# Laying the far group's stationary blocks out side by side before a value projection

## The chip, the cores and the metric

The kernel runs on one core of one Trainium2 chip. The metric is device microseconds of one execution, the median of three runs. The program is about 17,000 instructions on five engines: TensorE (PE in the profile, with its weight loads as PEld), VectorE (DVE), the activation engine (ACT), GpSimd (POOL) and SyncE (SP), which only issues transfers.

## The reference, cut to what matters

One layer of an encoder block: a half-step SwiGLU feed-forward, a token mixing of two attention branches, and a second half-step feed-forward. The change sits in the mixing, in the values of the dilated attention branch:

```python
proj = h @ w_in[l]
qa, ka, va, qb, kb, vb, gate_a, gate_b = jnp.split(proj, splits, axis=-1)
...
def to_res(a):     # group g has dilation 1, 4 or 16
    return a.reshape(B, L, dilation, H, Dh).transpose(0, 2, 3, 1, 4).reshape(B * dilation, H, L, Dh)
o, lse = _banded_attention(to_res(q), to_res(k), to_res(v), half, dilation, slopes)
```

There are 512 tokens, 1024 channels, and three dilated groups of four heads of width 64. The kernel treats the groups with dilation 4 and 16 alike: tokens are sorted by their number modulo 4, four blocks of 128 tokens. These two are the far group.

## The kernel before, in words

Every product is made in three passes. A float32 operand is split into a high part (rounded to the fast matmul type) and a low part (the rest), and `mm3` (lines 203 to 206) issues high x high, high x low and low x high into one PSUM bank.

The normalised activations `hn` lie in SBUF with channels on the partitions, as eight chunks k = 0 to 7 of 128 channels by 512 tokens, one set of high parts (`hn_hi`) and one of low parts (`hn_lo`).

The mixing (lines 1255 to 1534) runs in this order on PE:

- the neighbourhood branch's query and key products, its value projection, its scores and its weighted sums;
- six dilated pairs (lines 1379 and 1380): pair j multiplies the activations with a query piece and a key piece, 24 matmuls each, into one bank each. `qk_parts` (line 974) then reads both banks on ACT and DVE and writes split copies. For pairs 2 to 5 it works through the 128 partitions in two halves, one for each of two heads: for each half ACT writes a scaled query (line 993), DVE its rest (line 994), and twice ACT a high part and DVE a low part of the key (lines 113 and 114, called by `split`), and two copies across (lines 999 and 1000). The query bank is free after the second half's line 994, and the key bank after the second half's last line 114;
- the far value projection `v_far` (line 1042), here called the far stage: 8 chunks k, 4 token blocks n, 3 passes, so 96 matmuls of 512 columns into four banks. The stationary operand is `seen(1, ...)` (line 935), a view of 128 tokens that stand four apart in memory. Two chunks share a weight piece (`take()`);
- the near value projection `v_near` (line 1016), then 16 gate projections with the remaining attention work beside them, and the output products.

In and around the far stage PE also runs the far groups' scores, `scores_narrow` (line 1098): each of eight heads uses two banks in turn, each filled by two matmuls (line 1106) and read by DVE (line 1110, then line 1114 twice).

All PSUM accumulators come from one pool of eight banks (line 56). While the far stage runs, four are its accumulators. Two others hold the products of pair 5 until `qk_parts` has read them, and two are left. A score that needs a third bank must take one from pair 5.

SBUF tiles of 128x512 float32 come from a pool of 38 units (line 53); a new tile waits until the last reader of the unit's former tile has run. The weight pieces arrive as `raw` tiles by SP and are split by ACT (line 113, 128x1024) and DVE (line 114, 128x1024) a few pieces ahead of their use.

In this part of the mixing the order of instructions on each engine is not written out by hand. A scheduler places them when the program is built, by program order, priorities and its own estimate of when operands are there. Each engine then runs its list in that order: an instruction that waits holds all behind it. Elsewhere (the feed-forwards, the start, the end) the order is pinned.

Of the kernel before, what the change touches and what calls it, by code (L numbers as in the profile page):

```python
# [12 lines left out]
F32 = mybir.dt.float32  # L13
F32R = mybir.dt.float32r
# [6 lines left out]
P = 128  # L21
T = 512
D = 1024
NK = D // P
# [9 lines left out]
URGENT = 400  # L34
# [12 lines left out]
def block_kernel(ctx, tc, x, gains, weights, rpb_near, rpb_all, alibi0, alibi12, out):  # L47
    nc = tc.nc
# [12 lines left out]
    def unit(dt=F32, name="u"):  # L61
        return up.tile([P, 512], dt, tag="u", name=name)
# [9 lines left out]
    def bank(name="ps"):  # L72
        return pp.tile([P, 512], F32, tag="ps", name=name)
# [15 lines left out]
    hn_hi, hn_lo = Rows(0), Rows(1)  # L89
# [30 lines left out]
    state = {"used": False, "next": 0, "take": 0, "stop": EARLY + 2 * STD, "ahead": lambda: None}  # L120
# [56 lines left out]
    def cut(w, c, n):  # L177

        return [a[c // 512][:, c % 512:c % 512 + n] for a in w]

    def take(ahead=True):
        w = pieces.pop(state["take"])
        state["take"] += 1
        if ahead:
            fill(NPIECE - 1)
        return w
# [11 lines left out]
    def step(n=1):  # L198
        for _ in range(n):
            if pend:  # L200
                pend.popleft()()

    def mm3(o, sh, sl, mh, ml, start, stop, **kw):
        nc.tensor.matmul(o, sh, mh, start=start, stop=False, **kw)  # L204
        nc.tensor.matmul(o, sh, ml, start=False, stop=False, **kw)  # L205
        nc.tensor.matmul(o, sl, mh, start=False, stop=stop, **kw)  # L206

    def proj_into(o, w, lo=0, hi=T):
        for k in range(NK):
            mm3(o[:, lo:hi], *cut(w, k * P, P),  # L210
                hn_hi[:, k, lo:hi], hn_lo[:, k, lo:hi], k == 0, k == NK - 1)
# [10 lines left out]
    def pair(use, j, n=2):  # L222
        a = bank()
        proj_into(a, take())
        step(n)
        b = bank()
        proj_into(b, take())
        step(n)
        use(j, a, b)
# [705 lines left out]
    def seen(kind, ap):  # L935

        if kind == "na":
            return ap.rearrange("p (r c) -> p c r", r=8)
        if kind == 0:
            return ap  # L940
        return ap.rearrange("p (i c) -> p c i", c=4)
# [18 lines left out]
    def parts_for(paired):  # L960
        if paired:
            t = twin("pair")
            return [t[:, cs] for cs in halves]
        return unit(F32R, "a"), unit(F32R, "a")

    def shaped(dst, view):
        sh = view.shape
        if len(sh) == 2:
            return dst
        if len(sh) == 3:  # L970
            return dst.rearrange("p (a b) -> p a b", a=sh[1])
        return dst.rearrange("p (a b c) -> p a b c", a=sh[1], b=sh[2])
# [31 lines left out]
    def v_parts(ps, v=None):  # L1004
        v = unit(F32R) if v is None else v
        v4 = v.rearrange("p (h s d) -> p h s d", h=4, s=2)
        split(v4[:, :, 0, :], v4[:, :, 1, :], ps.rearrange("p (h d) -> p h d", h=4))
        return v4
# [7 lines left out]
    def v_near():  # L1016
# [22 lines left out]
            step()  # L1039
        return [vv[3]] + vv[:3]  # L1040

    def v_far():

        acc = [bank() for _ in range(4)]
        for k in range(NK):
            if k % 2 == 0:
                w = take()
            parts = [seen(1, a[:, k, :]) for a in (hn_hi, hn_lo)]
            for n in range(4):
                mm3(acc[n], parts[0][:, n], parts[1][:, n], *cut(w, (k % 2) * 512, 512), k == 0, k == NK - 1)  # L1050
            if k % 2:
                step(2 if k == 5 else 1)
        vv = [[], []]
        for n in range(4):
            both = parts_for(True)
            for i in range(2):
                vv[i].append(v_parts(acc[n][:, i * 256:(i + 1) * 256], both[i]))
        return vv
# [196 lines left out]
    def mixing(g):  # L1255
# [9 lines left out]
        def load_tables(us, n, src):  # L1265
            def one(i):
                u = unit(name="table")
                nc.sync.dma_start(u, src[:, i * 512:(i + 1) * 512])
                us.append(u)
            for i in range(n):  # L1270
                loads.append(lambda i=i: one(i))
# [52 lines left out]
        def joint(g):  # L1324
            u = unit(name="joint")
            j = u[:, 0:96].rearrange("p (t g h c) -> p t g h c", t=4, g=3, h=4)
            nc.scalar.dma_start(u[:, 0:96].rearrange("p (t e) -> p t e", t=4), st_views[g])
            nm, rc, s = [u[:, 96 + 16 * i:112 + 16 * i].rearrange("p (t h) -> p t h", t=4) for i in range(3)]
            e, ws = [u[:, 144 + 48 * i:192 + 48 * i].rearrange("p (g t h) -> p g t h", g=3, t=4) for i in range(2)]
            nc.vector.tensor_tensor(nm, j[:, :, 0, :, 0], j[:, :, 1, :, 0], op=ALU.min)  # L1330
            nc.vector.tensor_tensor(nm, nm, j[:, :, 2, :, 0], op=ALU.min)
            for i in range(3):
                nc.vector.tensor_tensor(e[:, i], nm, j[:, :, i, :, 0], op=ALU.subtract)
            nc.scalar.activation(e, e, AF.Exp)
            nc.vector.tensor_tensor(ws, e, j[:, :, :, :, 1].rearrange("p t g h -> p g t h"), op=ALU.mult)
            nc.vector.tensor_tensor(ws[:, 0], ws[:, 0], ws[:, 1], op=ALU.add)
            nc.vector.tensor_tensor(ws[:, 0], ws[:, 0], ws[:, 2], op=ALU.add)
            nc.vector.reciprocal(rc, ws[:, 0])
            nc.vector.tensor_tensor(s, rc, e[:, g], op=ALU.mult)
            scl[g] = s  # L1340
# [36 lines left out]
        load_tables(g_tab[2], 1, alibi12[:, :512])  # L1377
        load_tables(g_tab[3], 1, alibi12[:, 512:])
        for j in range(6):
            pair(g_use, j, 1)  # L1380
        pend.append(lambda: joint(1))
        vvb[1], vvb[2] = v_far()
        vvb[0] = v_near()
        step(len(pend))
# [26 lines left out]
        parts = {}  # L1411
# [111 lines left out]
        acc = o.acc["r"] + o.acc["q"], o.acc["c"] + o.acc["z"]  # L1523
# [141 lines left out]
    ffn(1, False, x_r)  # L1665
    state["sp"] = len(nc.cur_bb.bb.instructions)
    mixing(3)
    ffn(5, True, x_kept)
    ordered[-1].append(mark())
# [130 lines left out]
```

## Time and profile before

| | |
|---|---|
| median of three runs | 1069.71 us (1069.48 to 1070.3) |
| profiled execution, its own time | 1070.8 us |
| span of that execution in the trace | 1069.0 us |
| PE busy | 1061.0 us, 99% of the span |
| DVE, ACT, POOL busy | 871.1, 653.0, 193.1 us |
| granted TensorE clock | 0.998 |

The trace's clock counts from the start of the span. A row of the timeline gives start, duration, engine, line, operation, what it writes and reads, and the count; in square brackets stands the time that the engine sat idle before it and what ended that. Matmuls are pipelined: a row's duration (0.39 us for 512 columns) is longer than the distance to the next row's start (about 0.23 us), and it is the distance that counts. The far stage runs from 499.27 us to 524.5 us.

### The profile page before, as it was taken

The numbers are of one execution on the slowest core, as the hardware profiler recorded it, in microseconds if no ns is written. First come the engines' busy times: TensorE is split into PE (matmuls) and PEld (weight loads), VectorE is DVE, ScalarE is ACT, GpSimd is POOL, SyncE is SP. The second block draws the span as 40 slices with busy tenths as digits, with TensorE's granted clock in tenths as the row PEclk, the third lists the DMA queues.
The fourth block names the chain that finished last, engine by engine and source line by source line (L and its number), as shares of the span: only waits on it lengthen the run. The fifth ranks groups of instructions, "written<-read, shape, count | busy, mean of one in ns | idle before, by whom it ended". The sixth has DMA issues, their size and how long they took to land.

```text
span 1069.0 us, 17160 instructions
## 1 busy us (share of the span) xinstructions
PE 1061.0 (99%) x5955; PEld 926.4 (87%) x5955; DVE 871.1 (81%) x1694; ACT 653.0 (61%) x1348; POOL 193.1 (18%) x253
## 2 busy tenths in 40 slices
PE   9999999999999999999999999999999999999997
PEld 7898988998888988888988888889899899988886
DVE  7998999989987666676777644777998999989985
ACT  7656656566674655577766641366655566667671
POOL 4111211024334000000000001043311111124331
PEclk9999999999999999999999999999999999999999
DMA  9899987779993444322233239595947678869952
GB/s 331 188 231 234 235 206 200 197 182 264 248 311 118 154 158 164 116 68 74 80 89 97 79 106 308 148 199 186 286 100 197 158 198 204 216 203 234 217 195 79
DMA packets 98027, 193.95 MB, mean 181 GB/s; under 512 B 24338, under 2 KB 26898, under 8 KB 97939
## 3 DMA queue, kind: packets, MB, share of 16 engines
q1 hardware_dynamic: 69760, 138.37, 38.8%
q0 software_dynamic: 25488, 54.01, 28.3%
q8 instruction: 47, 0.77, 0.3%
q10 hardware_dynamic: 2690, 0.46, 0.2%
q14 instruction: 42, 0.34, 0.1%
HBM read 185.68 MB, written 9.68 MB: 183 GB/s over the span
## 4 chain that ended last, share of the span: by engine, by line
PE 92%; DMA 4%; DVE 2%; ACT 0%; issue 0%; SPq 0%; DVEq 0%; ACTq 0%
PE ps L204 10%; PE ps L206 10%; PE ps L205 10%; PE q L461 7%; PE q L206 6%; PE q L204 6%; PE q L205 6%; PE p L461 6%; PE q L464 4%; PE p L464 3%; PE c L206 2%; PE c L204 2%; PE c L205 2%; PE r L461 2%; PE r L204 1%; PE r L206 1%
## 5 line engine op out<-in xcount | busy, mean ns | idle before, releaser
L114 DVE TENSOR_TENSOR w<-raw,w 128x512 fp32r<-128x512 f32 (+1 forms) x142 | 129.8, 919 | 70.9 <-ACT w L113 68.2
L113 ACT CAST w<-t 128x512 fp32r<-128x512 f32 x160 | 98.0, 622 | 115.1 <-DVE t L410 62.6
L113 ACT CAST w<-raw 128x512 fp32r<-128x512 f32 (+1 forms) x142 | 114.1, 809 | 78.9 <-PE ps L205 31.9
L204 PE MATMUL ps<-hn,w 128*128 128x512 f32 (+1 forms) x360 | 136.5, 379 | 0.0
L206 PE MATMUL ps<-hn,w 128*128 128x512 f32 (+1 forms) x360 | 134.6, 374 | 0.0
L205 PE MATMUL ps<-hn,w 128*128 128x512 f32 (+1 forms) x360 | 134.3, 373 | 0.0
L114 DVE TENSOR_TENSOR w<-t,w 128x512 fp32r<-128x512 f32 x160 | 108.3, 685 | 1.0 <-ACT w L113 0.8
L404 POOL DMA_DIRECT2D t<-in_weights_dram x40 | 35.0, 875 | 286.1 <-DVE w L114 58.5
L206 PEld LDWEIGHTS ps<-hn,w 128*128 128x128 f32 x360 | 67.8, 188 | 12.7 <-DVE w L114 0.7
L204 PEld LDWEIGHTS ps<-hn,w 128*128 128x128 f32 x360 | 67.9, 189 | 11.4
L205 PEld LDWEIGHTS ps<-hn,w 128*128 128x128 f32 x360 | 67.9, 189 | 10.9
L461 PE MATMUL p<-v,w 128*128 128x512 f32 x272 | 73.1, 390 | 0.0
L113 ACT CAST w<-room 128x1024 fp32r<-128x1024 f32 x49 | 51.5, 1052 | 31.7 <-PE q L206 7.8
L114 DVE TENSOR_TENSOR w<-room,w 128x1024 fp32r<-128x1024 f32 x49 | 59.6, 1220 | 7.3 <-ACT w L113 4.1
L461 PE MATMUL q<-v,w 128*128 128x512 f32 x240 | 65.1, 392 | 0.0
L750 POOL DMA_DIRECT2D room<-in_weights_dram x7 | 6.1, 873 | 320.5 <-DMA room<-in_weights_dram 313.9
L461 PEld LDWEIGHTS p<-v,w 128*128 128x128 f32 x272 | 50.4, 188 | 10.2
L731 POOL DMA_DIRECT2D rows<-in_weights_dram x36 | 37.0, 1251 | 95.0 <-DVE w L114 61.6
L461 PEld LDWEIGHTS q<-v,w 128*128 128x128 f32 x240 | 43.0, 189 | 7.5
L113 ACT CAST w<-rows 128x512 fp32r<-128x512 f32 x62 | 36.0, 618 | 20.7 <-PE q L206 9.5
L206 PE MATMUL q<-hn,w 128*128 128x256 f32 x168 | 47.5, 283 | 0.0
L205 PE MATMUL q<-hn,w 128*128 128x256 f32 x168 | 47.5, 283 | 0.0
(334 smaller groups left out, 3066.0 us busy)
## 6 DMA issues: line engine op xcount, KB each, us to landing
raw<-in_weights_dram SPq DMA_DIRECT2D x94, 512.0 KB
t<-in_weights_dram SPq DMA_DIRECT2D x88, 256.0 KB
t<-in_weights_dram POOLq DMA_DIRECT2D x80, 256.0 KB, 5.7
room<-in_weights_dram SPq DMA_DIRECT2D x37, 512.0 KB
room<-in_weights_dram POOLq DMA_DIRECT2D x29, 512.0 KB, 11.9
w<-in_weights_dram SPq DMA_DIRECT2D x40, 256.0 KB
rows<-in_weights_dram POOLq DMA_DIRECT2D x36, 256.0 KB, 8.7
w<-in_weights_dram POOLq DMA_DIRECT2D x32, 256.0 KB, 9.1
```

Source lines behind the costliest of these rows:

```text
L113: nc.scalar.copy(hi, src)
L114: nc.vector.tensor_tensor(lo, src, hi.bitcast(F32), op=ALU.subtract)
L204: nc.tensor.matmul(o, sh, mh, start=start, stop=False, **kw)
L205: nc.tensor.matmul(o, sh, ml, start=False, stop=False, **kw)
L206: nc.tensor.matmul(o, sl, mh, start=False, stop=stop, **kw)
L404: nc.gpsimd.dma_start(t1, weights[gate][:, :512], accum_op=ALU.add)
L461: nc.tensor.matmul(to, high[k], mv[i][k][2], start=start and k == 0, stop=False, skip_group_check=True)
L464: nc.tensor.matmul(acc, low[k], mv[i][k][0], start=False, stop=k == 3, skip_group_check=True)
L731: nc.gpsimd.dma_start(u, block(*add, d)[:, cs], accum_op=ALU.add)
L750: nc.gpsimd.dma_start(to, self.block(*b, 0), accum_op=ALU.add)
```

## The change

A helper `far_copy` writes, for one chunk k, the two strided views out into two fresh units: the high part by GpSimd (`tensor_copy`), the low part by ACT (`copy`), each a 128x512 float32 read that steps four elements, and a side by side write. Both are given a higher priority in the scheduler. The helper is called once ahead of pair 4 and once ahead of pair 5 (chunks 0 and 1), and then once for each chunk inside `v_far`, for the chunk two ahead. The matmuls read the copies; their number and the values do not change. That makes 8 copies on GpSimd and 8 on ACT, 16 units more.

```diff
+    far_parts = deque()
+
+    def far_copy():
+        k = len(far_parts) + state.setdefault("far", 0)
+        if k < NK:
+            us = []
+            for a, copy in ((hn_hi, nc.gpsimd.tensor_copy), (hn_lo, nc.scalar.copy)):
+                view, u = seen(1, a[:, k, :]), unit(F32R)
+                with tc.high_priority(offset=URGENT):
+                    copy(shaped(u, view), view.bitcast(F32))
+                us.append(u)
+            far_parts.append(us)
+
     def v_far():
 
         acc = [bank() for _ in range(4)]
         for k in range(NK):
             if k % 2 == 0:
                 w = take()
-            parts = [seen(1, a[:, k, :]) for a in (hn_hi, hn_lo)]
+            far_copy()
+            high, low = far_parts.popleft()
+            state["far"] += 1
             for n in range(4):
-                mm3(acc[n], parts[0][:, n], parts[1][:, n], *cut(w, (k % 2) * 512, 512), k == 0, k == NK - 1)
+                mm3(acc[n], high[:, n * P:(n + 1) * P], low[:, n * P:(n + 1) * P], *cut(w, (k % 2) * 512, 512), k == 0, k == NK - 1)
             if k % 2:
                 step(2 if k == 5 else 1)
...
         for j in range(6):
+            if j > 3:
+                far_copy()
             pair(g_use, j, 1)
```

The changed program is the same on every engine up to and after the mixing. Inside it the scheduler has placed PE, DVE and ACT differently around the far stage. Lines below 1042 keep their numbers; behind that the changed kernel's lines are 15 higher (line 1106 becomes 1121, 1110 becomes 1125, 1114 becomes 1129), and behind its second edit 17.

On PE, before, near the third and fourth bank of scores. `ps_5895` to `ps_5898` are the four accumulators, `ps_5979` and `ps_5988` the third and fourth score bank, `hn_4038` and `hn_4039` the activations; "waits" names the engines whose signal a row waits for:

```order
L204 MATMUL ps_5898<-w_5589,hn_4038 128x512
L205 MATMUL ps_5898<-w_5590,hn_4038 128x512
L206 MATMUL ps_5898<-w_5589,hn_4038 128x512
L1106 MATMUL ps_5979<-k_5461,q_5460 128x256 [waits DVE_49,PE_49]
L1106 MATMUL ps_5979<-k_5461,q_5460 128x256
L204 MATMUL ps_5895<-w_5649,hn_4039 128x512
L205 MATMUL ps_5895<-w_5650,hn_4039 128x512
L206 MATMUL ps_5895<-w_5649,hn_4039 128x512
```

48 matmuls of the far stage (chunks 0 to 3) stand ahead of the third score bank, and six more between it and the fourth. The first two banks stand after 32.

The same place on PE now. `u_5718` and `u_5720` are the copies of chunk 1, `u_5913` of chunk 2, `ps_5903` to `ps_5906` the accumulators, and the score banks from the first to the fifth are `ps_5946`, `ps_5955`, `ps_6003`, `ps_6012` and `ps_6060`:

```order
L206 MATMUL ps_5906<-w_5520,u_5720 128x512
L1121 MATMUL ps_5946<-k_5450,q_5449 128x256 [waits DVE_49]
L1121 MATMUL ps_5946<-k_5450,q_5449 128x256
L1121 MATMUL ps_5955<-k_5451,q_5449 128x256 [waits DVE_49]
L1121 MATMUL ps_5955<-k_5451,q_5449 128x256
L1121 MATMUL ps_6003<-k_5461,q_5460 128x256 [waits DVE_49,PE_49]
L1121 MATMUL ps_6003<-k_5461,q_5460 128x256
L1121 MATMUL ps_6012<-k_5462,q_5460 128x256 [waits DVE_49,PE_49]
L1121 MATMUL ps_6012<-k_5462,q_5460 128x256
L1121 MATMUL ps_6060<-k_5565,q_5564 128x256 [waits DVE_49,PE_49]
L1121 MATMUL ps_6060<-k_5565,q_5564 128x256
L204 MATMUL ps_5903<-w_5593,u_5913 128x512 [waits Pool_49]
```

24 matmuls of the far stage (chunks 0 and 1) stand ahead of all five score banks, and chunk 2 behind them. The third bank still waits for pair 5's second line 994 and the fourth for pair 5's last line 114.

On DVE, before, between those two. `q_5884` is that line 994, `k_5886` that last line 114, `w_5951` the split of a weight piece:

```order
L994 SCALAR_TENSOR_TENSOR q_5884<-ps_5714,q_5884 64x512
L114 TENSOR_TENSOR k_5885<-ps_5793,k_5885 64x256
L999 CAST k_5885<-k_5885 64x512
L1110 TENSOR_TENSOR low_5933<-ps_5930,table_5227 128x256
L1114 ISA u_5929,st_4161<-ps_5930,low_5933 128x128
L1114 ISA st_4161 128x1
L1114 ISA u_5929,st_4161<-ps_5930,low_5933 128x128
L1114 ISA st_4161 128x1
L1110 TENSOR_TENSOR low_5942<-ps_5939,table_5227 128x256
L114 TENSOR_TENSOR w_5951<-raw_5948,w_5950 128x1024
L114 TENSOR_TENSOR k_5886<-ps_5793,k_5886 64x256
```

The same on DVE now, with `q_5892`, `k_5894` and `w_5967` in their places:

```order
L994 SCALAR_TENSOR_TENSOR q_5892<-ps_5722,q_5892 64x512
L114 TENSOR_TENSOR w_5967<-raw_5964,w_5966 128x1024
L114 TENSOR_TENSOR k_5893<-ps_5801,k_5893 64x256
L999 CAST k_5893<-k_5893 64x512
L1125 TENSOR_TENSOR low_5949<-ps_5946,table_5227 128x256
L114 TENSOR_TENSOR k_5894<-ps_5801,k_5894 64x256
L1129 ISA u_5945,st_4161<-ps_5946,low_5949 128x128
```

The weight split stands ahead of both key splits now, and the score work between is one row instead of six. On ACT the order up to the second line 993 is as before, but for one copy of chunk 1 ahead of the preceding line 1000; behind it the weight cast (line 113, 128x1024) comes first, then line 1000 and two key casts, and then the copies of chunks 2 and 3. On GpSimd the eight copies stand one behind the other; that of chunk 2 waits for the 21st matmul of the far stage, that of chunk 3 for the 24th, and that of chunk 4 for the first two line 1129 after `k_5894`, all for the release of a unit.

## The prediction

> **What bounds the kernel now.** I read the page first, then what TensorE waited for, then the stretches around the far stage. Page, sections 1 and 4:
>
> ```profile
> span 1069.0 us, 17160 instructions
> PE 1061.0 (99%) x5955; PEld 926.4 (87%) x5955; DVE 871.1 (81%) x1694; ACT 653.0 (61%) x1348; POOL 193.1 (18%) x253
> PE 92%; DMA 4%; DVE 2%; ACT 0%; issue 0%; SPq 0%; DVEq 0%; ACTq 0%
> ```
>
> The waits of PE over the whole span, and the busy time by stretches (columns PE, PEld, DVE, ACT, POOL, clock, DMA share, GB/s):
>
> ```profile
> PE warm L1577 <- DVE idle L1541: 1.2, 1, 1.2
> PE q L461 <- DVE p L506: 0.3, 1, 0.3
> ...
> 499.00:525.00 26.00, 26.00 (x123) 25.62 (x122) 18.84 (x71) 18.71 (x64) 0.00 (x0) 1.00 0.27 82
> 525.00:697.00 172.00, 172.00 (x874) 146.83 (x873) 112.19 (x260) 86.62 (x166) 8.29 (x11) 1.00 0.46 135
> ```
>
> PE makes up 92% of the chain that ended last, and behind the start it waits 0.3 us at most. In and after the far stage it is busy without a gap. So each microsecond that PE loses or gains there reaches the end, and nothing behind catches it up. GpSimd is idle in the far stage, ACT and DVE are 72% busy.
>
> What the strided reading costs shows in the weight loads (mean ns last but one), far stage first, then a pair, and in the starts of first and last matmuls of a run without other work, a pair's and then the far stage's:
>
> ```profile
> L204 PEld LDWEIGHTS ps<-w,hn 128*128 128x128 f32 x32 | 9.9, 310 | 0.1
> ...
> L204 PEld LDWEIGHTS ps<-hn,w 128*128 128x128 f32 x8 | 1.5, 188 | 0.4
> ...
> 451.70 0.40 PE L204 MATMUL ps<-hn,w 128*128 128x512 f32 x1
> ...
> 456.25 0.39 PE L206 MATMUL ps<-hn,w 128*128 128x512 f32 x1
> ...
> 520.28 0.40 PE L204 MATMUL ps<-w,hn 128*128 128x512 f32 x1
> ...
> 524.28 0.39 PE L206 MATMUL ps<-w,hn 128*128 128x512 f32 x1
> ```
>
> A load takes 310 instead of 188 ns, but the next load runs beside the matmul. From start to start the pair needs 4.55 us for 20 steps, 0.2275 us each, the far stage 4.00 us for 17, 0.2353 us. Only 0.0078 us of the 0.122 us shows.
>
> **The change, part by part.** *Side by side loads.* 96 matmuls x 0.0078 = 0.75 us gained, if the distance falls to the pair's.
>
> *The order on PE.* This is the term that decides. Here is where PE stood before when it came to the score banks:
>
> ```profile
> 499.27 0.63 PE L204 MATMUL ps<-w,hn 128*128 128x512 f32 x1
> 499.73 0.40 PE L205 MATMUL ps<-w,hn 128*128 128x512 f32 x1
> ...
> 507.02 0.64 PE L1106 MATMUL ps<-k,q 128*128 128x256 f32 x4
> 507.50 0.51 PE L204 MATMUL ps<-w,hn 128*128 128x512 f32 x1
> 507.85 0.40 PE L205 MATMUL ps<-w,hn 128*128 128x512 f32 x1
> ...
> 511.37 0.40 PE L1106 MATMUL ps<-k,q 128*128 128x256 f32 x2
> ...
> 513.12 0.40 PE L1106 MATMUL ps<-k,q 128*128 128x256 f32 x2
> ```
>
> And here is DVE in that time, with pair 5's second line 994, the work behind it, and pair 5's last line 114 at 510.39; and of ACT the line 993 ahead of that 994, a key cast and the weight cast:
>
> ```profile
> 506.23 0.69 DVE L994 SCALAR_TENSOR_TENSOR q<-ps,q 64x512 fp32r<-64x512 f32 x1 [0.20 <-ACT q L993]
> 507.01 0.43 DVE L114 TENSOR_TENSOR k<-ps,k 64x256 fp32r<-64x256 f32 x1
> 507.47 0.42 DVE L999 CAST k<-k 64x512 fp32r<-64x512 f32 x1
> 507.93 0.42 DVE L1110 TENSOR_TENSOR low<-ps,table 128x256 f32<-128x256 f32 x1
> 508.38 0.29 DVE L1114 CUSTOM_DVE_ANT_0 u<-ps,low 128x128 f32<-128x128 f32 x1
> ...
> 509.15 1.22 DVE L114 TENSOR_TENSOR w<-raw,w 128x1024 fp32r<-128x1024 f32 x1
> 510.39 0.43 DVE L114 TENSOR_TENSOR k<-ps,k 64x256 fp32r<-64x256 f32 x1
> ...
> 505.60 0.59 ACT L993 ACTIVATE q<-ps 64x512 fp32r<-64x512 f32 x1
> ...
> 507.00 1.05 ACT L113 CAST w<-raw 128x1024 fp32r<-128x1024 f32 x1
> 508.07 0.37 ACT L113 CAST k<-ps 64x256 fp32r<-64x256 f32 x1
> ```
>
> Before, the third score bank (511.37) came 4.45 us after its release, the end of line 994 at 506.92; the fourth (513.12) 2.3 us after its own, at 510.82. Both waits were covered by the far stage's matmuls that stood ahead. Now 24 stand ahead instead of 48.
>
> Arrival: 499.27, plus 0.23 for the first step (0.46 instead of 0.235), plus 24 x 0.2275 = 5.46, gives 504.96; four score matmuls add 0.48 (507.02 to 507.50). PE reaches the third bank at 505.44. ACT and DVE have the same rows ahead of line 994 as before, so it ends at 506.92 again: **wait 1.5 us**. The third bank's two matmuls take half of those 0.48, 0.24: from 506.92 PE is at the fourth at 507.16.
>
> Release of the fourth: ACT ends line 993 at 506.19 and casts the weight piece to 507.24 (1.05); DVE then splits it to 508.46 (1.22), key split 0.43, line 999 0.42, score sum 0.42, last key split 0.43: 510.16, with at most 0.16 less if a second reader of a bank overlaps its forerunner (the rows at 507.47, 507.93 and 508.38 do not: they start 0.46 and 0.45 apart at 0.42 each). I take 510.0. **Wait 2.85 us.** PE is at the fifth bank at 510.25; that is the first bank again, which DVE reads twice behind the last key split (0.29 each, 0.08 of it overlapping): 510.5. **Wait 0.25 us.** Sum 4.6.
>
> Bounds: 1.4 to 2.7 for the first wait (if the one ACT copy ahead delays the chain by its whole length, below), 2.6 to 3.05 for the second, 0.15 to 0.3 for the third.
>
> *Fewer alternations.* Coming back from scores costs the first matmul 0.35 (507.50 to 507.85) instead of 0.235. Before, the far stage was broken five times; now three times. 2 x 0.115 = 0.2 gained; bounds 0 and 0.35.
>
> *ACT's copies.* No row shows this shape. The nearest are a cast of the same operand over 128x384 with a wide step and a plain 128x512 cast; with them stands ACT's idle time just where the copy of chunk 1 is put, ahead of line 1000:
>
> ```profile
> L1012 ACT CAST u<-hn 128x384 fp32r<-128x384 f32 x8 | 7.4, 926 | 0.0
> ...
> L113 ACT CAST pair<-h 128x512 fp32r<-128x512 f32 x3 | 1.9, 618 | 0.0
> ...
> 493.13 0.62 ACT L1000 CAST k<-k 64x512 fp32r<-64x512 f32 x1 [1.36 <-DVE k L114]
> ```
>
> Between 0.62 (no penalty) and 1.24 (926 ns x 512/384); I take 1.2, since the source is the same and steps too. It fits the 1.36 us that ACT waits there, so it costs nothing. If that cover went, 1.2 would go to the first wait. The copies of chunks 2 and 3 stand behind the last key casts, are done by about 509.2 + 1.2 = 510.4 and 511.6, and PE reads the first at about 511.
>
> *GpSimd's copies.* Nearest rows: a subtraction of the same size with both inputs plain, and beside it a small operation of GpSimd twice, once while DVE ran a weight split:
>
> ```profile
> 10.89 1.30 POOL L1614 TENSOR_TENSOR w<-raw,w 128x512 fp32r<-128x512 f32 x1 [0.21 <-ACT w L1613]
> 13.88 0.28 POOL L303 TENSOR_SCALAR ms<-ssx,ms 128x1 f32<-128x1 f32 x1 [0.41 <-ACT junk L292]
> ...
> 16.20 1.34 POOL L303 TENSOR_SCALAR ms<-ssx,ms 128x1 f32<-128x1 f32 x1 [0.61 <-ACT junk L292]
> ...
> 16.17 1.22 DVE L114 TENSOR_TENSOR w<-raw,w 128x1024 fp32r<-128x1024 f32 x1
> ```
>
> Bounds 0.65 (one input instead of two, half) and 2.6 (twice, as ACT's wide step costs); I take 1.3. Those of chunks 0 and 1 run long before 499. Chunk 2's waits for the 21st far matmul, about 504.4, chunk 3's follows: done at 507.0, needed at about 510.75 and 513.5. The last four start at about 510.5 and the fourth of them is needed at about 525.1: they are hidden up to 3.65 us each, above both bounds.
>
> Sum: 4.6 - 0.75 - 0.2 = +3.65, with bounds +3.0 and +5.9. The profiled execution of 1070.8 us becomes 1074.45, the median of 1069.71, which lies 1.1 lower, 1073.4.
>
> **The rivals.** *The banks are free in time* (not slower). Place: the third and fourth score bank. If DVE has read pair 5 by 505.4 and 507.2, no wait arises: -0.95, 1068.8 us. For it speaks that ACT and DVE are a quarter idle in the stage; against it that the end of line 994 hangs on rows that the change leaves in place, seven exponentials of ACT ahead of line 993, and the weight split that is now ahead of the last key split. It decides from 4.6 us of earlier release on. Chance 0.10.
>
> *GpSimd holds DVE.* L303 took 0.28 us alone and 1.34 beside the weight split, ending 0.15 us after it: one engine was held by the other. Turned round, the copies of chunks 2 and 3 run from 504.4; if each takes 2.6 they last to 509.6 and the weight split, due at 507.24, starts 2.35 later, on the fourth bank's path: +6.0, 1075.7 us. Below 1.4 us a copy they are out of the way in time. [...] Chance 0.15.
>
> *GpSimd sets the pace.* From 3.65 us a copy on, PE waits for chunks 3 to 7. At 5 us the chunks come 5 instead of 2.75 us apart: chunk 3 at 514.4, then four more and a last one at 534.4 instead of 525.1, +9.3 on top: 1082.7 us. No row is near. Chance 0.04.
>
> That side by side loads don't shorten the distance (it has another reason) is possible too; it takes 0.75 away, 1074.2 us, and lies inside the forecast.
>
> **How the numbers follow.** The forecast of 1073.4 us has the rest, 0.71, with its own range of 1072.7 to 1075.6. The range over cases is 1071.6 to 1076.2: it takes the second rival in at its price, allows the first wait to be smaller by 1.1 us, and leaves out the first and third rival and tails. A measurement can tell about 0.2%, 2.1 us: faster is below 1067.6, slower above 1071.85. Faster needs three times what there is to gain: 0.02. Same is the first rival and a small tail: 0.13. Slower 0.85.
>
> **What would show it.** Right: PE idle in front of line 1121 twice in the far stage, once released by line 994 (about 1.5 us) and once by line 114 (about 2.85), far loads at about 188 ns, distances of 0.2275 us, GpSimd copies under 2 us. Wrong: no wait of PE there, or waits in front of line 204 released by GpSimd; DVE's weight split starting well after ACT's cast has ended.

## The result and the profile after

| | before | changed |
|---|---|---|
| median of six runs each | 1070.14 us (1069.48 to 1071.74) | 1076.4 us (1075.39 to 1077.44) |
| profiled execution, its own time | 1070.8 us | 1076.39 us |
| span of that execution | 1069.0 us | 1074.5 us |

The ratio is 1.0056, with a 95% interval from 1.0045 to 1.0067: slower by 6.0 us, where +3.65 was forecast. On the median of before that the forecast used, 1069.71, the ratio gives 1075.7 us, near the upper end of the range.

The page of the changed kernel, its span and the chain that ended last:

```profile
span 1074.5 us, 17194 instructions
...
PE 95%; ACT 2%; DMA 1%; DVE 1%; issue 1%; SPq 0%; DVEq 0%; ACTq 0%
```

TensorE's waits over the whole span (total, times, longest):

```profile
PE ps L1121 <- DVE k L114: 3.0, 1, 3.0
PE ps L1121 <- DVE q L994: 2.1, 1, 2.1
```

The kernel before has no such rows. They name the two places of the forecast, the third score bank (released by pair 5's second line 994) and the fourth (released by its last line 114). The timeline of TensorE around them:

```profile
498.83 0.50 PE L204 MATMUL ps<-w,u 128*128 128x512 f32 x1
...
504.18 0.39 PE L206 MATMUL ps<-w,u 128*128 128x512 f32 x1
504.40 0.63 PE L1121 MATMUL ps<-k,q 128*128 128x256 f32 x4
507.11 0.47 PE L1121 MATMUL ps<-k,q 128*128 128x256 f32 x2 [2.07 <-DVE q L994]
510.54 1.31 PE L1121 MATMUL ps<-k,q 128*128 128x256 f32 x4 [2.96 <-DVE k L114]
511.65 0.63 PE L204 MATMUL ps<-w,u 128*128 128x512 f32 x1
512.08 0.63 PE L205 MATMUL ps<-w,u 128*128 128x512 f32 x1
...
514.51 0.39 PE L205 MATMUL ps<-w,u 128*128 128x512 f32 x1
...
516.59 0.39 PE L204 MATMUL ps<-w,u 128*128 128x512 f32 x1
...
523.87 0.39 PE L206 MATMUL ps<-w,u 128*128 128x512 f32 x1
...
530.51 0.28 PE L204 MATMUL ps<-w,hn 128*128 128x256 f32 x1
```

Three things stand here. First the two waits, 2.07 and 2.96 us. Then something that the forecast did not have: behind the waits the matmuls of 512 columns start 0.43 us apart (511.65 to 512.08), and only from 514.51 on as usual. Last the gain: from 516.59 to 523.87 there are 32 steps, 0.2275 us each, as forecast for side by side loads.

The busy time by stretches (the column behind the engines is the granted TensorE clock) tells what the slow steps are:

```profile
505.00:507.50 2.50, 0.43 (x3) 0.30 (x2) 1.60 (x4) 2.43 (x6) 1.28 (x2) 1.00 0.11 7
507.50:514.30 6.80, 3.83 (x12) 3.17 (x12) 4.55 (x15) 5.83 (x12) 2.20 (x2) 0.50 0.24 77
514.30:525.00 10.70, 10.70 (x51) 8.95 (x50) 4.76 (x21) 8.91 (x25) 2.16 (x2) 1.00 0.14 51
```

From 507.5 to 514.3 the clock was granted at 0.50. TensorE worked in it from 510.54 on, 3.77 us at half speed, which costs half of that, 1.9 us. The clock fell at 507.50, before the second wait began (at 507.58, the end of the row at 507.11): the first wait brought it down, and the second came while it was down.

The bill of the far stage, from its first step to the first matmul of 256 columns behind it: 31.68 us now (498.83 to 530.51). Before, it was 25.72, from 499.27 to this row of the timeline of before:

```profile
524.99 0.28 PE L204 MATMUL ps<-w,hn 128*128 128x256 f32 x1
```

That is +5.96. To set the forecast's terms against it, the waits must be counted as the forecast counts them, from step to step; the time in square brackets starts later, at the modelled end of the row before. Four score matmuls from 504.40 take 0.48, so the first wait runs from 504.88 to 507.11, 2.23 us. The third bank's two take 0.24, so the second runs from 507.35 to 510.54, 3.19 us. Waits 5.42 and half clock 1.9 make 7.32, and 1.36 us was gained: 0.75 by the loads, and about 0.6 because coming back from scores costs nothing now (0.23 us from 515.89 to the next step at 516.12, where before it cost 0.35, five times). The span grew by 5.5 only, since this execution came to the far stage 0.44 us earlier (498.83 instead of 499.27). It had that lead long ahead of the first copy; the last score matmuls of an early pair, before and after:

```profile
400.97 1.69 PE L1134 MATMUL ps<-k,q 64*128 64x256 f32 x24
```

```profile
400.53 1.69 PE L1149 MATMUL ps<-k,q 64*128 64x256 f32 x24
```

The lead made the first wait longer by as much and changes nothing behind it.

### The profile page after: what moved, and what is told of

It reads as the page before. It is cut to its first block, busy times and chain, and to the rows that moved or that the text cites. A ratio compares the mean times of both kernels' runs of the same rounds, so it can differ in the third digit from the quotient of the medians.

```text
span 1074.5 us, 17194 instructions
## 1 busy us (share of the span) xinstructions
PE 1061.2 (99%) x5955; PEld 922.6 (86%) x5955; DVE 872.1 (81%) x1694; ACT 659.4 (61%) x1354; POOL 195.1 (18%) x261
## 4 chain that ended last, share of the span: by engine, by line
PE 95%; ACT 2%; DMA 1%; DVE 1%; issue 1%; SPq 0%; DVEq 0%; ACTq 0%
PE ps L204 10%; PE ps L206 10%; PE ps L205 10%; PE q L461 8%; PE q L206 7%; PE q L204 7%; PE q L205 7%; PE p L461 6%; PE q L464 4%; PE p L464 3%; PE r L461 2%; PE c L206 2%; PE c L204 2%; PE c L205 2%; PE r L204 1%; PE r L205 1%
## 5 line engine op out<-in xcount | busy, mean ns | idle before, releaser
L731 POOL DMA_DIRECT2D rows<-in_weights_dram x36 | 34.5, 1161 | 93.2 <-DVE w L114 62.0
L205 PE MATMUL q<-hn,w 128*128 128x256 f32 x168 | 47.5, 283 | 0.0
L206 PE MATMUL q<-hn,w 128*128 128x256 f32 x168 | 47.5, 283 | 0.0
L204 PE MATMUL q<-hn,w 128*128 128x256 f32 x168 | 47.5, 283 | 0.0
```

The source lines that it names most:

```text
L731: nc.gpsimd.dma_start(u, block(*add, d)[:, cs], accum_op=ALU.add)
```

## The experiments

The theory: TensorE's new order (24 far matmuls, then score banks) makes it wait for pair 5's two banks, and standing still brings its clock to half. The rivals: the copies themselves cost the time (on the activation engine, or on GpSimd by holding DVE), or the slow steps come from two engines copying beside TensorE.

### High parts alone

```diff
-            for a, copy in ((hn_hi, nc.gpsimd.tensor_copy), (hn_lo, nc.scalar.copy)):
+            for a, copy in ((hn_hi, nc.gpsimd.tensor_copy),):
...
-            high, low = far_parts.popleft()
+            high, low = far_parts.popleft()[0], seen(1, hn_lo[:, k, :])
...
-                mm3(acc[n], high[:, n * P:(n + 1) * P], low[:, n * P:(n + 1) * P], *cut(w, (k % 2) * 512, 512), k == 0, k == NK - 1)
+                mm3(acc[n], high[:, n * P:(n + 1) * P], low[:, n], *cut(w, (k % 2) * 512, 512), k == 0, k == NK - 1)
```

> Only the high parts are copied (by GpSimd, chunks 0 and 1 ahead as in the change); the low parts are read from the strided view again, and the activation engine copies nothing. The order on TensorE keeps its flaw: 24 far matmuls, then five score banks, then chunk 2. Theory (the order makes TensorE wait for pair 5's two banks, and the waits bring the clock to half): the same two waits in front of line 1121, about 2.1 us behind line 994 and 2.7 to 3.0 us behind line 114, and again some 3.6 us at half clock behind them; 64 instead of 96 side by side loads give 0.25 us less. 1076.5 us, 1075.8 to 1077.2. Rival (the activation engine's copies hold up what TensorE waits for): the waits shrink with the copies gone, and the time falls below 1073. Rival (GpSimd's copies hold DVE, 6.0 us): the same 1076.5, so this run does not speak on it.

Measured: 1076.94 us, ratio 1.0065 (1.0052 to 1.0077). The waits and the clock:

```profile
PE ps L1121 <- DVE k L114: 3.3, 1, 3.3
PE ps L1121 <- DVE q L994: 1.5, 1, 1.5
```

```profile
509.00:515.70 6.70, 5.70 (x15) 4.72 (x16) 4.44 (x26) 4.58 (x21) 2.23 (x2) 0.50 0.19 73
```

The time stays without one copy on the activation engine, so that rival falls. The half clock now covers 5.7 us of work (2.85 us lost), and the waits are about 0.2 us shorter in sum. The second alone is 0.3 us longer than in the changed kernel (3.28 against 2.96), because GpSimd held DVE ahead of the last key split: behind one of its copies line 999 took 0.74 instead of 0.42 us. That copy itself took 1.87 instead of 1.1 us, since it began while DVE ran the weight split (506.48 to 507.71).

```profile
506.79 1.87 POOL L1051 CAST u<-hn 128x512 fp32r<-128x512 f32 x1 [0.87 <-PE ps L1121]
508.20 0.74 DVE L999 CAST k<-k 64x512 fp32r<-64x512 f32 x1
```

### High parts alone, four chunks ahead

```diff
-            if j > 3:
+            if j > 1:
                 far_copy()
```

> As the run with high parts alone, but copied four chunks ahead (once ahead of each of pairs 2 to 5) instead of two, so that the copies take as many units as the change's do. GpSimd makes the same eight copies. The scheduler then leaves TensorE in nearly the order of before: 32 far matmuls, two banks, 16, the third bank, 11, the fourth. Theory (order and waits): no wait in front of line 1121, clock 1.00 throughout; 64 side by side loads at 0.0078 us less each: 0.5 us below before, 1069.6 us, 1068.9 to 1070.4. Rival (GpSimd's copies hold DVE wherever they run, or the copies cost by being made): some of the 6 us stays, 1072 or more.

Measured: 1069.18 us, ratio 0.9994 (0.9985 to 1.0003), not to be told apart from before and 7.8 us under the run above, whose code differs from it only in how far ahead the copies are made, and which gets another order by it. TensorE comes to the third and fourth bank late, as before, and the rows carry no wait; the stretch that was at half clock is at full:

```profile
510.49 0.40 PE L1121 MATMUL ps<-k,q 128*128 128x256 f32 x2
...
513.30 0.40 PE L1121 MATMUL ps<-k,q 128*128 128x256 f32 x2
```

```profile
509.00:515.70 6.70, 6.70 (x33) 5.90 (x32) 6.10 (x26) 4.51 (x17) 2.18 (x2) 1.00 0.29 83
```

The eight GpSimd copies cost TensorE nothing here. They do hold DVE, though; a key copy and the weight split while GpSimd copied from 506.37 to 508.75:

```profile
506.97 0.81 DVE L999 CAST k<-k 64x512 fp32r<-64x512 f32 x1
...
508.16 1.68 DVE L114 TENSOR_TENSOR w<-raw,w 128x1024 fp32r<-128x1024 f32 x1
```

Both took 0.4 to 0.5 us longer than before (0.42 and 1.22), and nobody waited for it.

### The order without the copies

On the kernel before, with TensorE's instructions of the far stage pinned in the order in which they are written (`pool` holds the stretches to pin). `step(n)` puts in the scores of n heads; the call with two heads moves from chunk 5 to chunk 1:

```diff
+        begin = mark()
         acc = [bank() for _ in range(4)]
...
-                step(2 if k == 5 else 1)
+                step(2 if k == 1 else 1)
+        pool.append((begin, mark(), (mybir.EngineType.PE,)))
```

> The kernel before, without any copy, with one thing changed: TensorE's order within the far stage is pinned to 24 far matmuls, four score banks, 24, two banks, 24, two, 24, two. Theory (the order alone costs the time): waits at the third bank (0.1 to 0.5 us: without the wait's forerunners the activation engine may come to line 993 earlier) and at the fourth (2.7 to 3.0 us), +3.0 us without the clock; if the clock falls to half as it did in the changed kernel, 1.8 us more. 1074.9 us, or 1073.1 if a single wait of 2.9 us is too short for the clock to fall. Rival (the copies cost the time, not the order): 1070.1 us.

Measured: 1076.87 us, ratio 1.0067 (1.0055 to 1.008), 2 us more than expected. No copy is made, and the whole loss is there:

```profile
PE ps L1108 <- DVE k L114: 3.0, 1, 3.0
PE ps L1108 <- DVE q L994: 1.2, 1, 1.2
```

```profile
507.40:514.20 6.80, 4.57 (x12) 3.77 (x13) 4.82 (x24) 4.18 (x18) 0.00 (x0) 0.50 0.23 77
```

The first wait was expected too short (0.1 to 0.5 us; it was 1.2), and the half clock costs 2.3 us instead of 1.8. What costs the time in the changed kernel is the order; the copies act there by making the scheduler choose another one. On DVE the weight split stands ahead of both key splits here too, as in the changed kernel. That is not what costs the time: the last key split ended at 510.40 in the changed kernel and at 510.82 in the kernel before, so the fourth bank came free no later than it used to.

### Both waits filled with work

On the changed kernel:

```diff
-            for i in range(2):
+            for i in [0, 1] * (again.popleft() if again else 1):
                 k = ks[b].rearrange("p (s n t) -> p n s t", s=2, n=2)[:, i]
...
+        again.extend((1, 9, 12))
         acc = [bank() for _ in range(4)]
```

> The changed kernel, with the second score bank's two matmuls issued nine times and the third's twelve times, into the same bank with the same result, so that TensorE works where it waited: 16 more matmuls of 256 columns ahead of the third bank (1.9 us) and 22 ahead of the fourth (2.6 us). Everything else stands as in the changed kernel up to the fifth bank, and nothing of the result is left out. Theory (the halved clock from 507.5 to 514.2 follows from TensorE standing idle, and costs 1.8 us): the granted clock stays at 1.00, the steps of 0.427 us behind the fifth bank become 0.2275, 1074.6 us, 1074.0 to 1075.2. Rival (those steps are slow because GpSimd and the activation engine copy at the same time): they stay slow, 1076.4 us. [...]

Measured: 1074.6 us, ratio 1.0042 (1.0029 to 1.0056), as expected. The repeated matmuls fill the two waits, and the steps behind them are at full speed:

```profile
504.51 2.55 PE L1123 MATMUL ps<-k,q 128*128 128x256 f32 x20
507.22 3.11 PE L1123 MATMUL ps<-k,q 128*128 128x256 f32 x24 [0.15 <-DVE q L994]
510.65 1.02 PE L1123 MATMUL ps<-k,q 128*128 128x256 f32 x4 [0.33 <-DVE k L114]
511.51 0.40 PE L204 MATMUL ps<-w,u 128*128 128x512 f32 x1
511.74 0.39 PE L205 MATMUL ps<-w,u 128*128 128x512 f32 x1
```

```profile
507.50:514.30 6.80, 6.39 (x41) 5.57 (x40) 4.75 (x15) 5.83 (x12) 2.16 (x2) 1.00 0.24 77
```

GpSimd (2.16 us) and the activation engine (5.83) are as busy in this stretch as in the changed kernel (2.20 and 5.83), so their copying does not make the steps slow: standing still does, by 1.8 us between the medians (1.5 by the ratios).

### One wait filled, the other left

The same edit with `(1, 9, 1)`, which leaves the wait at the fourth bank, and with `(1, 1, 12)`, which leaves that at the third.

> As the run with both waits filled, but only the first of them: the second score bank's two matmuls are issued nine times, the third's once, so the wait of 3 us at the fourth bank is left. [...] Theory: the wait of 3 us alone mostly makes such a stretch, the clock falls for 3.4 to 6.8 us and costs 1.7 us or somewhat more, 1076.2 us, 1075.2 to 1077.2. Rival (it takes both waits together): clock 1.00, 1074.6 us as with both filled.

Measured: 1076.47 us, ratio 1.0058 (1.0045 to 1.0071), as expected. In the profiled execution the wait of 3 us alone was enough:

```profile
508.80:515.70 6.90, 5.50 (x15) 4.53 (x16) 2.97 (x13) 6.77 (x14) 2.19 (x2) 0.51 0.23 76
```

The 3.4 us of half clock and the 1.7 us that it costs were the author's estimate, which no run before this one shows; here TensorE worked for 5.5 us at half clock, which costs 2.75.

> Only the second wait is filled: the third score bank's two matmuls are issued twelve times, the second's once, so the wait of 2.1 us at the third bank is left. Theory (a stretch of 3.4 us with over 2 us of standing still makes the clock fall, and where the stretches begin changes from run to run): it falls in about 4 of 10 executions, since the whole wait must lie in one stretch; median 1074.6 us with some executions 1.5 to 3 us above it. Rival (any wait of 2 us makes it fall): all of them 1076 or more. Rival (no wait under 3 us does): all of them within 0.6 us of 1074.6.

Measured: 1074.75 us (1074.03 to 1075.34), ratio 1.0042 (1.003 to 1.0055). The executions lie within 0.75 us of 1074.6, without the outliers of 1.5 to 3 us that were expected, and none reaches 1076. But the times hardly tell the theories apart, since most of the slow steps fell on the repeated matmuls, which stand in for a wait: from the third bank to the far stage took 4.91 us (507.06 to 511.97), only 0.6 more than with both waits filled (507.22 to 511.51). The trace does tell: the clock fell after a wait of 2.06 us.

```profile
507.06 5.07 PE L1123 MATMUL ps<-k,q 128*128 128x256 f32 x28 [2.06 <-DVE q L994]
```

```profile
508.40:511.90 3.50, 3.50 (x19) 3.50 (x18) 2.75 (x10) 2.79 (x4) 0.89 (x1) 0.51 0.48 150
```

The clock fell at 508.4, 1.4 us after TensorE had begun to work again, and came back 3.4 us later. That the clock is decided in stretches, and the 4 of 10 that the theory works out from them, were the author's estimate and are not shown; the trace shows a single piece of half clock, 3.41 us long. All three traces in which TensorE came to a wait of 2.05 to 2.07 us at full clock (the changed kernel, this run and the last one below) show the fall; how often such a wait does it stays open.

### The order as the code is written

The changed kernel with TensorE pinned as in the third experiment, but with its `step` calls left as they are:

```diff
+        begin = mark()
         acc = [bank() for _ in range(4)]
...
+        pool.append((begin, mark(), (mybir.EngineType.PE,)))
```

> The changed kernel with all its copies, and TensorE's order in the far stage pinned as the code is written: 24 far matmuls, two score banks, 24, two, 24, four, 24, two. Theory (order and waits): no wait at the third and fourth bank, but the low copy of chunk 2, which stands behind the key casts on the activation engine (509.50 in the changed kernel), is now late: one wait of about 3.1 us in front of line 206, and mostly some 1.7 us of halved clock behind it. 2.3 + 1.7 us above before, 1074.0 us, 1072.2 to 1075.2. Rival (the loss hangs on the score banks alone, the copies are early enough): 1069.2 us.

Measured: 1075.72 us, ratio 1.0051 (1.0038 to 1.0064). The score banks make no wait, and the low copy of chunk 2 makes one that is longer than expected:

```profile
504.83 0.40 PE L205 MATMUL ps<-w,u 128*128 128x512 f32 x1
509.78 0.79 PE L206 MATMUL ps<-w,u 128*128 128x512 f32 x1 [4.55 <-ACT u L1051]
```

The expectation took the copy to be done about 1.4 us earlier than it was. So holding TensorE to the written order does not rescue the change: with the activation engine's list as it is, chunk 2 is really late. No run has all sixteen copies without a wait, so that they would be free under another order is not shown. The expectation's 1.7 us of halved clock was the author's estimate as well: TensorE worked at half clock from 509.78 to 514.42, 4.64 us, which costs 2.3.

### The same with both copies on GpSimd

```diff
-            for a, copy in ((hn_hi, nc.gpsimd.tensor_copy), (hn_lo, nc.scalar.copy)):
+            for a, copy in ((hn_hi, nc.gpsimd.tensor_copy), (hn_lo, nc.gpsimd.tensor_copy)):
```

> The same pinned order, and both copies of each chunk made by GpSimd (16 copies of 1.1 us), none by the activation engine. Theory: chunk 2's two copies start when a unit comes free at about 504 and are done 2.3 us later, a little after TensorE wants them; two or three waits of 0.2 to 0.5 us in front of line 206, clock 1.00, 96 side by side loads at 0.0078 us less: 0.3 us below before, 1069.8 us, 1068.9 to 1070.8. Rival (GpSimd holds DVE): GpSimd copies from 504 to 508.5 without a break, so DVE's weight split, due at 507.3, starts only at 508.5, the key splits behind it free the fourth bank 1.2 us later than TensorE comes to it, and the time is 1071 or more.

Measured: 1073.42 us, ratio 1.003 (1.0019 to 1.0041); the expectation missed, and the rival's time came out by another way. TensorE loses only 0.3 us at chunk 2 (a step of 0.52 us at 504.86) and waits for no score bank. It waits for chunk 4, whose copies start only at 512.02: 2.05 us for the high part and 0.31 for the low one.

```profile
513.18 0.50 PE L204 MATMUL ps<-w,u 128*128 128x512 f32 x1 [2.05 <-POOL u L1051]
```

```profile
504.23 3.21 POOL L1051 CAST u<-hn 128x512 fp32r<-128x512 f32 x3 [1.41 <-PE ps L205]
512.02 9.39 POOL L1051 CAST u<-hn 128x512 fp32r<-128x512 f32 x8 [4.58 <-PE ps L1123]
```

```profile
514.70:518.20 3.50, 3.50 (x10) 2.71 (x9) 0.98 (x5) 0.88 (x4) 3.50 (x3) 0.51 0.49 149
```

GpSimd itself stood idle for 4.58 us ahead of these copies: the next free unit hung on the score work. The row names TensorE's score matmuls, but these had ended by 511.14; which later reader of the unit released it is not shown. The half clock follows this wait too. And DVE was held here: its weight split took 2.07 us where it takes 1.22 otherwise. That is 0.85 us, and TensorE had no wait at a score bank.

```profile
506.45 2.07 DVE L114 TENSOR_TENSOR w<-raw,w 128x1024 fp32r<-128x1024 f32 x1 [0.39 <-ACT w L113]
```

## Why the prediction was right in sign and short in size

- **The order on TensorE decides: right.** The order without copies has the whole loss (1.0067), and eight copies, all on GpSimd, without that order have none (0.9994).
- **The first wait, 1.5 us: 2.23 from step to step, 2.07 in the row.** 0.44 of the difference is the lead with which this execution came; 0.15 is the time from the end of line 994 (506.27 + 0.69 = 506.96) to TensorE's start at 507.11, which the forecast had set to zero, and 0.12 a faster first step (0.34 instead of 0.46).
- **The second wait, 2.85 us: 3.19 from step to step, 2.96 in the row.** The chain ran as written down, weight split, key split, line 999, score sum, key split. It ended at 510.40 where the forecast took 510.0, and TensorE started 0.14 later:

```profile
506.27 0.69 DVE L994 SCALAR_TENSOR_TENSOR q<-ps,q 64x512 fp32r<-64x512 f32 x1 [0.20 <-ACT q L993]
507.34 1.23 DVE L114 TENSOR_TENSOR w<-raw,w 128x1024 fp32r<-128x1024 f32 x1 [0.38 <-ACT w L113]
508.59 0.43 DVE L114 TENSOR_TENSOR k<-ps,k 64x256 fp32r<-64x256 f32 x1
...
509.97 0.43 DVE L114 TENSOR_TENSOR k<-ps,k 64x256 fp32r<-64x256 f32 x1
```

- **The third wait, 0.25 us: none.** The fourth bank's two matmuls ran at half clock, and the first bank was free by the time that they had.
- **The sum of 4.6 for the waits was the step that failed.** It priced a wait at its length alone. The waits also brought the granted clock to 0.50 for 6.8 us, of which TensorE worked 3.77: 1.9 us more, and 1.5 to 1.8 by the run with the waits filled. No row of before prices a wait between matmuls, because behind the start TensorE never stood still for more than 0.3 us. But its trace has slow steps at the start: the same matmul takes 0.65 us at 6.31 and 0.38 at 7.32, and the clock's first recorded change, to full, lies at 7.00. These matmuls are called `warm` (line 1577, issued by `keep_warm`) and do nothing but keep TensorE at work; the list of waits that the forecast quotes names them, and the forecast passed over them.

```profile
6.31 0.65 PE L1577 MATMUL warm<-idle 128*128 128x512 bf16 x1
...
7.32 0.38 PE L1577 MATMUL warm<-idle 128*128 128x512 bf16 x1
```

- **Side by side loads, -0.75: right; fewer alternations, -0.2: too small.** 0.2275 us a step was measured, and the two together gained 1.36 instead of 0.95.
- **That the time lies inside the stated range is in part luck.** The forecast's own case ends at 1075.6, and 1075.7 is above it. The range reaches 1076.2 only because it takes in the rival that GpSimd holds DVE at its price of 6.0 us, while the time came about by another mechanism. The forecast's own upper bound of +5.9 was also too high for its terms: the bounds of the waits add up to 6.05, and the 0.75 of the loads leaves 5.3.
- **The copies' durations were about right and were hidden.** Forecast were 1.3 us on GpSimd and 1.2 on the activation engine; the groups of the changed kernel:

```profile
L1051 POOL CAST u<-hn 128x512 fp32r<-128x512 f32 x8 | 8.9, 1136 | 163.5 <-DVE u L1228 139.9 <-PE ps L206 16.0 <-issue 4.8
L1051 ACT CAST u<-hn 128x512 fp32r<-128x512 f32 x8 | 8.7, 1112 | 0.1
```

- **The rival that GpSimd holds DVE gave nearly the measured time, 1075.7, for a reason that did not act here.** It put the weight split 2.35 us late; the split started at 507.34, 0.03 us after the activation engine's cast had ended at 507.31, and took its usual 1.23. What was held is an earlier copy of line 999, 1.33 instead of 0.42 us while GpSimd copied from 503.95 to 506.28. DVE waited for the activation engine behind it anyway:

```profile
504.00 1.33 DVE L999 CAST k<-k 64x512 fp32r<-64x512 f32 x1
505.65 0.42 DVE L114 TENSOR_TENSOR k<-ps,k 64x256 fp32r<-64x256 f32 x1 [0.32 <-ACT k L113]
```

## What to carry to other kernels

A change that gives a scheduler new work with late operands can cost more by the order that comes out than by the work; compare the order of the busiest engine first, and ask of each instruction that moved forward whether its buffer is free by then. In these traces the waits of 2.05 us or more on a TensorE that is otherwise never idle, alone or close to another, cost their length and brought 1.7 to 2.9 us of half clock behind them, unless the slow steps fell on work that can be spared. A gain of 0.0078 us per matmul, 0.75 us in all, leaves no room for one such wait.

## What the runs showed of the hardware

**The half clock came in pieces of two lengths.** By the changes of the clock that the traces record, it lasted 6.83 us in five (changed kernel, high parts alone, order without copies, first wait filled, written order) and 3.41 us in two (second wait filled, both copies on GpSimd). A fall can come after the wait is over (1.56 us after, 513.18 to 514.74, in the last run). In the changed kernel the 3.41 us ahead of the fall, 504.09 to 507.50, hold the first wait, and TensorE worked for 39% of them; in the next 3.41 us it worked for 13%, and behind those from 510.92 to 514.33, full of work, the clock came back. In the seven traces TensorE had worked for 14 to 51% of the 3.41 us ahead of the fall, and all through the 3.41 us ahead of the return; in high parts alone it worked for 67% of the time from 508.86 to 512.28, and the clock stayed at half. What decides between fall and return beyond that is not shown.

All six executions of the changed kernel have a mean granted clock of 0.995, against 0.998 in the profiled one of before. In the order without copies, the first wait filled, the written order and both copies on GpSimd it differs between executions, by 0.002 to 0.003, so the half clock that the one profiled execution shows need not be the same in the others.

**GpSimd and DVE hold each other.** Beside GpSimd's copies, DVE's copies of line 999 took 0.74 (high parts alone), 0.81 (four chunks ahead) and 1.33 us (changed kernel) instead of 0.42, and its weight splits 1.68 (four chunks ahead) and 2.07 (both copies on GpSimd) instead of 1.22, while the key splits from PSUM kept their 0.42 to 0.43. The other way round, a GpSimd copy that began beside a weight split took 1.87 instead of 1.1 (high parts alone). By what means the one holds the other is not shown.
